# Layer 1's gated mixer: one output tile behind each block of products instead of two behind each pair

## The chip, the cores and the metric

The kernel is one program on one core of one Trainium2 chip. TensorE (PE) multiplies, with its weight loads shown apart as PEld; VectorE (DVE), ScalarE (ACT) and GpSimd (POOL) work on tiles in the on-chip memory SBUF and on the accumulators in PSUM; SyncE (SP) issues the DMA transfers from and to the device memory. Each engine takes its instructions in the order in which the program wrote them, and waits for other engines on semaphores. The metric is the device time of one execution in microseconds (us).

## The reference

The reference is one inference step of a two-layer trunk for 1024 prompt tokens and 8 x 8 = 64 sample tokens that share the weights, all in float32. Each layer has a token mixer and behind it a gated channel mixer (SwiGLU). The part that the change touches is the channel mixer of layer 1:

```
h = h + swiglu(rms_norm(h, norm_ffn_g[layer]), w_ffn_in[layer], w_ffn_out[layer])

def swiglu(h, w_in, w_out):
    g, u = jnp.split(h @ w_in, 2, axis=-1)
    return (jax.nn.silu(g) * u) @ w_out
```

The model width is 1024 and the hidden width 2816, which is 22 blocks of 128 hidden rows. Everything before it (attention with a paged cache, convolutions, pooling, layer 0's mixer) stays as it is.

## The kernel before

**Precision.** A float32 operand is kept as two parts that TensorE multiplies fast, a high part (a rounded copy, made by ACT) and a low part (the rest, a subtraction by POOL or DVE). A product takes three matmuls per 128 rows of the contraction: high weight times high data, high weight times low data, low weight times high data. So the low part of a weight is first read by the third matmul of a product.

**Groups.** The tokens run through layer 1's mixer in two groups, A (512 tokens, `GA`) and B (576 tokens, `GB`), one after the other, by `channel1`, which calls `run_ffn` (L456). Activations lie with channels on partitions and tokens along the free axis. The running sum `hb` stays in SBUF.

**A block of products.** For one block of 128 hidden rows, gate and up part together are a 2 x 2 block product, and `strassen` (L513) computes it with seven half-size products instead of eight. They go into four PSUM accumulators in this order: X (two products), Y (two), Z (two), W (one). Each product is 4 x 3 = 12 matmuls of 256 (A) or 288 (B) columns, so a block is 84. Seven adds on DVE (L525), an ACT copy (L537) and a Silu on ACT (L550) put the results together. `gated` leaves behind a POOL product of gate and up (L500) and a split of the result `hid` into high and low part (L240 on ACT, L241 on DVE); these are kept in the lists `post` and `late`, and `flush()` writes what is in them into the program.

**An output tile.** The hidden rows of two blocks are multiplied with a slice of `w_ffn_out` of 256 x 512: four quarter tiles of 128 output channels (`out_block`), each with its own accumulator, and behind each an add into `hb` (L295, `added`). The second slice covers the other 512 channels. Before the change, both output tiles of pair q-1 follow the two blocks of pair q. Three accumulators go round.

**Weights.** `loads` and `seq` hold the order in which weights are fetched and used; `add_ffn` writes that order for the channel mixer. SP fetches each slice into one of four `stage` buffers (L166). `w_split` turns them into `hl` tiles (three go round), which hold high and low parts. A block has four such entries r = 0 to 3, with seven half-tiles in all: for r = 0 DVE first makes three sums of gate and up weights (L200, L201, L202), then ACT and POOL cut them (L196, L197); r = 1 and 2 cut one more of the sums and three pieces of the fetched weights; r = 3 cuts one more sum (`sum_c`, L214). An output slice is cut in one piece by ACT and two by POOL (L184, L186). `w_next` hands out the next entry and splits ahead to two entries behind it:

```
    def w_next(live=0):
        j = wj[0]
        wj[0] += 1
        w_split(j + 3 - live)
        w_load(need(j + 6 - live))
```

While `thin[0]` is set, the three sums of an r = 0 entry aren't written at once but put into `parts_`, to be written one at a time.

**Side work.** `slot()` is called at fixed places, and every third call writes a piece of other work: in group A, pieces of group B's norm (L1683, DVE), in group B the squares of the finished tokens of A (L251 on ACT, L252 on POOL) and their final norm and output (L1881).

Of the kernel before, what the change touches and what calls it, by code (L numbers as in the profile page):

```python
# [22 lines left out]
NF = FFN // 128  # L23
# [34 lines left out]
def trunk_kernel(ctx, tc, x_prompt, x_sample, cache_k, cache_v, state_conformer, state_shortconv, state_pool,  # L58
# [19 lines left out]
    def tmp():  # L78
        return tmpbox[0].tile([128, tmpbox[1]], F, name="tmp")
# [15 lines left out]
    hb = hpool.tile([128, KC, T], F, name="hb")  # L95
# [9 lines left out]
    def add_load(src, kt):  # L105
        loads.append((src, kt))
        return len(loads) - 1

    def in_load(w, c0):
        return add_load(w.rearrange("(k p) n -> p k n", p=128)[:, :, c0:c0 + 128], 8)  # L110

    def add_in(w, c0):
        seq.append((in_load(w, c0), None, 0))

    def add_out(w, g, o):
        seq.append((add_load(w.rearrange("(k p) n -> p k n", p=128)[:, 2 * g:2 * g + 2, o * 512:o * 512 + 512], 2),
                    None, 0))

    def add_ffn(l, plain, both=True):
        for g in range(NF // 2):  # L120
            for f in (2 * g, 2 * g + 1):
                if f < plain:
                    add_in(w_ffn_in[l], f * 128)
                    add_in(w_ffn_in[l], FFN + f * 128)
                else:
                    a = in_load(w_ffn_in[l], f * 128), in_load(w_ffn_in[l], FFN + f * 128)
                    seq.extend(a + (r,) for r in range(4))
            if g and (g < NF // 2 - 1 or not both):
                for o in range(2):
                    add_out(w_ffn_out[l], g - 1, o)  # L130
        for o in range(2):
            if both:
                add_out(w_ffn_out[l], NF // 2 - 2, o)
            add_out(w_ffn_out[l], NF // 2 - 1, o)
# [38 lines left out]
    sums, parts_, thin = {}, [], [False]  # L173
# [46 lines left out]
    wj = [0]  # L220
# [6 lines that stand above are left out]
        return hls.pop(j)  # L227
# [65 lines left out]
    def added(g, dst, acc):  # L293
        for a, d in parts(g, acc, dst):
            dve.tensor_tensor(d, a, d, op=OP.add)  # L295
# [5 lines left out]
    def flush():  # L301
        todo = post + late
        post.clear()
        late.clear()
        for f in todo:
            f()
# [120 lines left out]
    def out_block(g, a, h, i, hh, first=True, last=True):  # L427
        for k in range(2):
            mm3(g, a, h[:, 0, k, i * 128:i * 128 + 128], h[:, 1, k, i * 128:i * 128 + 128], hh[:, k],
                first and k == 0, last and k == 1)  # L430
# [25 lines left out]
    def run_ffn(g, accs, ps, hidp, x, last, sig=False, slot=lambda: None, forms=None, plain=NF,  # L456
                free=lambda: None, hw=None, both=True):
        G = NF // 2
        n = g.n
        hid = {}  # L460
        gate = {}
        done = forms and "switch" not in forms

        def ev_g(a):
            t = tmp()
            if done:
                for p, o in parts(g, a, t):
                    act.activation(o, p, AF.Silu)
                gate["t"] = t
                return  # L470
            scaled(g, t[:, :n], a)
            if sig:
                s = tmp()
                act.activation(s[:, :n], t[:, :n], AF.Sigmoid)
                pool.tensor_tensor(t[:, :n], t[:, :n], s[:, :n], op=OP.mult)
            else:
                act.activation(t[:, :n], t[:, :n], AF.Silu)  # L477
            gate["t"] = t

        def to_hid(f):  # L480
            if f // 2 not in hid:
                hid[f // 2] = hidp.tile([128, 2, 2, hw or n], FR, name="hid")[:, :, :, :n]
            return hid[f // 2][:, f % 2]

        def ev_u(f, a):
            if done:
                t, dst = gate.pop("t"), to_hid(f)
                for p, o in parts(g, a, t):
                    dve.tensor_tensor(o, p, o, op=OP.mult)
                late.append(lambda: split(dst, t[:, :n]))  # L490
                return
            t = tmp()
            scaled(g, t[:, :n], a)
            gated(f, t, gate.pop("t"))

        def gated(f, t, u):
            dst = to_hid(f)

            def fin():
                (dve if both and f == NF - 1 else pool).tensor_tensor(t[:, :n], t[:, :n], u[:, :n], op=OP.mult)  # L500
                late.append(lambda: split(dst, t[:, :n], on=pool if sig else None))
            post.append(fin)

        def one(f, which):
            h = w_next()
            a = accs()
            block(g, a, h, x, K0[4:] + K0[:4] if done else K0, slot=slot)
            flush()
            ev_g(a) if which == 0 else ev_u(f, a)
            slot()  # L510

        def strassen(f):
            w2 = n // 2

            def prod(acc, h, i, b):
                for k in range(4):
                    xk = forms[b](k)
                    for s, (wi, xi) in enumerate(((0, 0), (0, 1), (1, 0))):  # L520
                        pe.matmul(acc[:, :w2], h[:, wi, i, k], xk[:, xi], start=k == 0 and s == 0,  # L521
                                  stop=k == 3 and s == 2)

            def add(out, acc, x):
                dve.tensor_tensor(out, acc[:, :w2], x, op=OP.add)  # L525

            a, b = slice(0, w2), slice(w2, n)
            X, h = accs(), w_next()
            prod(X[:, 0], h, 0, "t2")
            prod(X[:, 1], h, 1, "t3")  # L530
            flush()
            slot()
            Y, h = accs(), w_next()
            prod(Y[:, 0], h, 0, "t1")
            prod(Y[:, 1], h, 1, "b11")
            G_, U, P = tmp(), tmp(), tmp()
            act.activation(G_[:, a], Y[:, 1, :w2], AF.Copy)  # L537
            Z, h = accs(), w_next()
            prod(Z[:, 0], h, 0, "t4")
            add(U[:, a], X[:, 0], G_[:, a])  # L540
            add(U[:, b], X[:, 1], U[:, a])
            add(P[:, b], Y[:, 0], U[:, b])
            add(G_[:, b], Y[:, 0], U[:, a])
            prod(Z[:, 1], h, 1, "b21")
            W, h = accs(), w_next()
            prod(W[:, 0], h, 0, "b22")
            add(P[:, a], Z[:, 0], U[:, b])
            add(G_[:, a], Z[:, 1], G_[:, a])
            add(G_[:, b], W[:, 0], G_[:, b])
            act.activation(G_[:, :n], G_[:, :n], AF.Silu)  # L550
            gated(f, P, G_)
            slot()

        for q in range(G + 1):
            if q < G:
                for f in (2 * q, 2 * q + 1):
                    if f >= plain:
                        if f == plain:
                            forms.get("switch", forms.get("ready"))()
                        strassen(f)  # L560
                        continue
                    if f == 0 and not done:
                        run_in(g, accs, x, [ev_g, lambda a: ev_u(0, a)], norm_hooks(g, ps, at=(4, 7)), skew=3)
                        slot()
                        continue
                    one(f, 0)
                    one(f, 1)
            if q == G - 1:
                free()
                if both:  # L570
                    return last([hid.pop(q - 1), hid.pop(q)])
            if q == G:
                flush()
                flush()
                last(hid.pop(q - 1))
            elif q:
                hh = hid.pop(q - 1)
                for o in range(2):
                    thin[0] = True
                    h = w_next()  # L580
                    thin[0] = False
                    for i in range(4):
                        a = accs()
                        out_block(g, a, h, i, hh)
                        added(g, hb[:, o * 4 + i, g.cs], a)
                        if parts_:
                            parts_.pop(0)()
                        if o == 0 and i == 1:
                            flush()
                        slot()  # L590
# [45 lines left out]
    def accs():  # L636
        return accbox["p"].tile([128, len(accbox["g"].blocks), 512], F, name="acc")
# [1100 lines left out]
    for n in range(2, KC):  # L1738
        h = w_next()
        a = accs()  # L1740
# [4 lines left out]
    with tc.tile_pool(name="fab", bufs=1) as ep:  # L1745
        gen = forms_a(ep)
        for n in range(KC):
            h = w_next()
            a = accs()
# [256 lines left out]
```

## Time and profile before

| what | value |
|---|---|
| median of 3 runs | 2517.12 us (2516.61 to 2517.3) |
| profiled execution | 2522.03 us |
| its span, first to last instruction | 2519.8 us |
| mean granted TensorE clock | 0.992 |
| busy: PE / PEld / DVE / ACT / POOL | 96 / 87 / 66 / 44 / 64% of the span |
| moved by DMA | 258.32 MB, mean 103 GB/s |
| layer 1's channel mixer, group A, about | 1723 to 2103 us |
| the same, group B, about | 2103 to 2489 us |

In the rows that are shown below, L235 is the line of the helper that writes most matmuls (output tiles included), L521 that of the block products. A row of the timeline is start, duration, engine, line, operation, written tile <- read tiles, shapes, count, and in brackets the idle time of the engine just before it with what ended it. A row of the waits is: engine, tile and line that waited <- what it waited for: total us, times, longest. A row of the chain is start, duration, engine, tile and line. A row of the windows is the stretch, its length, then the busy time of PE, PEld, DVE, ACT and POOL (with counts), the granted clock, the DMA engines' busy share and GB/s.

### The profile page before, as it was taken

How to read it: one execution, taken by the hardware profiler on the slowest of the kernel's cores; microseconds unless marked ns; L12 is line 12 of the kernel's file. 1: busy time of each engine (PE TensorE's matmuls, PEld its weight loads, DVE VectorE, ACT ScalarE, POOL GpSimd, SP SyncE). 2: the span in 40 equal slices, each digit the busy share in tenths (PEclk: the TensorE clock that was granted, in tenths of full speed). 3: DMA queues.
4: the chain of work that ended last, by engine and by line, in shares of the span. 5: the costliest groups of instructions: out<-in, count | busy, mean ns of one | idle time of the engine just before them, and what ended most of it. 6: DMA issues, size and time to landing. Idle time of an engine off the chain costs nothing.

```text
span 2519.8 us, 41443 instructions
## 1 busy us (share of the span) xinstructions
PE 2427.2 (96%) x15871; PEld 2192.4 (87%) x15871; DVE 1664.8 (66%) x2301; ACT 1106.7 (44%) x1875; POOL 1619.5 (64%) x1263
## 2 busy tenths in 40 slices
PE   8999999999999999999999999998999999999998
PEld 6788877788777679999999899888888888999997
DVE  3696878977777653767565533458777679666655
ACT  5536776754444343343334422234333444443333
POOL 6664343655554576777778523267888886887775
PEclk9999999999999999999999999999999999999999
DMA  7332241234665534223232311252233333233322
GB/s 224 116 108 72 76 113 45 72 111 136 184 179 159 159 92 147 78 66 101 85 101 85 107 51 42 68 141 68 84 101 101 94 92 92 84 97 114 92 84 80
DMA packets 355486, 258.32 MB, mean 103 GB/s; under 512 B 22913, under 2 KB 303617, under 8 KB 355272
## 3 DMA queue, kind: packets, MB, share of 16 engines
q1 hardware_dynamic: 355256, 255.66, 34.5%
q8 instruction: 126, 2.06, 0.3%
q14 instruction: 72, 0.59, 0.1%
q10 hardware_dynamic: 32, 0.01, 0.0%
HBM read 237.41 MB, written 18.69 MB: 102 GB/s over the span
## 4 chain that ended last, share of the span: by engine, by line
PE 43%; DVE 10%; POOL 3%; issue 2%; ACT 1%; POOLq 0%; DVEq 0%; ACTq 0%
PE acc L235 22%; PE acc L521 19%; DVE sum L200 2%; POOL hl L197 2%; DVE hb L295 1%; DVE hid L241 1%; DVE sum L201 1%; DVE sum L202 1%; DVE b L1686 0%; DVE tmp L525 0%; POOL tmp L500 0%; DVE sum_c L214 0%; DVE fb L1690 0%; PE blk L1909 0%; DVE x L1686 0%
## 5 line engine op out<-in xcount | busy, mean ns | idle before, releaser
L186 POOL TENSOR_TENSOR hl<-stage,hl 128x512 fp32r<-128x512 f32 x464 | 633.7, 1390 | 395.7 <-ACT hl L184 287.4
L235 PE MATMUL acc<-x,hl 128*128 128x512 f32 (+1 forms) x3648 | 774.3, 350 | 12.9 <-DVE tmp L291 3.0
L235 PEld LDWEIGHTS acc<-x,hl 128*128 128x128 f32 x3648 | 588.3, 190 | 77.7 <-issue 6.2
L235 PE MATMUL acc<-hid,hl 128*128 128x288 f32 (+1 forms) x3096 | 550.3, 333 | 13.0 <-DVE hb L295 5.5
L235 PEld LDWEIGHTS acc<-hid,hl 128*128 128x128 f32 x3096 | 471.5, 190 | 66.7 <-DVE hb L295 7.9
L295 DVE TENSOR_TENSOR hb<-acc,hb 128x512 f32<-128x512 f32 (+1 forms) x360 | 256.2, 718 | 175.2 <-PE acc L235 174.1
L521 PE MATMUL acc<-x,hl 128*128 128x288 f32 (+1 forms) x2676 | 362.2, 290 | 3.4 <-POOL hl L197 2.3
L521 PEld LDWEIGHTS acc<-x,hl 128*128 128x128 f32 x2676 | 349.0, 188 | 5.7 <-POOL hl L197 3.1
L197 POOL TENSOR_TENSOR hl<-sum,hl 128x512 fp32r<-128x512 f32 x180 | 237.2, 1346 | 176.3 <-ACT hl L196 176.3
L184 ACT ACTIVATE hl<-stage 128x1024 fp32r<-128x1024 f32 x232 | 243.4, 1054 | 229.3 <-PE acc L235 140.5
L525 DVE TENSOR_TENSOR tmp<-acc,tmp 128x288 f32<-128x288 f32 (+1 forms) x420 | 173.6, 442 | 230.3 <-ACT tmp L537 135.3
L197 POOL TENSOR_TENSOR hl<-stage,hl 128x512 fp32r<-128x512 f32 x180 | 268.5, 1514 | 13.0 <-ACT hl L196 12.9
L521 PE MATMUL acc<-b,hl 128*128 128x256 f32 (+1 forms) x1548 | 216.5, 291 | 14.9 <-DVE tmp L525 12.0
L521 PEld LDWEIGHTS acc<-b,hl 128*128 128x128 f32 x1548 | 202.2, 189 | 20.5 <-ACT hl L196 12.9
L235 PE MATMUL acc<-x1t,hl 128*128 128x288 f32 x1152 | 216.3, 296 | 1.5 <-POOL hl L186 1.5
L235 PEld LDWEIGHTS acc<-x1t,hl 128*128 128x128 f32 x1152 | 195.9, 188 | 19.5 <-POOL hl L186 1.7
L196 ACT ACTIVATE hl<-sum 128x512 fp32r<-128x512 f32 x180 | 103.1, 623 | 242.2 <-DVE sum L202 219.4
L291 DVE TENSOR_TENSOR tmp<-acc,rr 128x512 f32<-128x512 f32 (+1 forms) x108 | 75.2, 710 | 139.7 <-PE acc L235 122.6
L196 ACT ACTIVATE hl<-stage 128x512 fp32r<-128x512 f32 x180 | 105.5, 618 | 67.8 <-PE acc L235 62.7
L500 POOL TENSOR_TENSOR tmp<-tmp 128x576 f32<-128x576 f32 (+1 forms) x85 | 125.6, 1477 | 9.3 <-ACT tmp L477 8.3
L252 POOL TENSOR_TENSOR ss<-ss,tmp 128x512 f32<-128x512 f32 (+1 forms) x69 | 107.0, 1551 | 29.0 <-ACT tmp L251 18.8
L235 PE MATMUL acc<-x1a,hl 128*128 128x512 f32 x480 | 122.4, 409 | 2.9 <-POOL hl L186 1.3
(293 smaller groups left out, 3177.4 us busy)
## 6 DMA issues: line engine op xcount, KB each, us to landing
stage<-in_w_ffn_in_dram SPq DMA_DIRECT2D x176, 512.0 KB
stage<-in_w_ffn_out_dram SPq DMA_DIRECT2D x88, 512.0 KB
stage<-in_w_in_even_dram SPq DMA_DIRECT2D x40, 512.0 KB
kst<-in_cache_k_dram SPq DMA_DIRECT2D x64, 256.0 KB
vst<-in_cache_v_dram SPq DMA_DIRECT2D x56, 256.0 KB
stage<-in_w_out_even_dram SPq DMA_DIRECT2D x16, 512.0 KB
stage<-in_w_in_odd_dram SPq DMA_DIRECT2D x16, 512.0 KB
stage<-in_w_out_odd_dram SPq DMA_DIRECT2D x16, 512.0 KB
```

Source lines behind the costliest of these rows:

```text
L184: act.activation(hl[:, 0], st, AF.Copy)
L186: pool.tensor_tensor(hl[:, 1, c], st[:, c], f32(hl[:, 0, c]), op=OP.subtract)
L196: act.activation(hl[:, 0, c], x, AF.Copy)
L197: pool.tensor_tensor(hl[:, 1, c], x, f32(hl[:, 0, c]), op=OP.subtract)
L200: todo = [lambda: dve.tensor_tensor(sb, su[:, lo], su[:, hi], op=OP.add), lambda: dve.tensor_tensor(sa[:, hi], sg[:, lo], su[:, lo], op=OP ...
L235: pe.matmul(acc[:, b, :c1 - c0], w, xs[:, xi, c0 - o:c1 - o], start=first and s == 0, stop=last and s == 2)
L252: pool.tensor_tensor(ss[:, g.cs], ss[:, g.cs], t[:, :g.n], op=OP.add)
L291: dve.tensor_tensor(d, a, r, op=OP.mult)
L295: dve.tensor_tensor(d, a, d, op=OP.add)
L500: (dve if both and f == NF - 1 else pool).tensor_tensor(t[:, :n], t[:, :n], u[:, :n], op=OP.mult)
L521: pe.matmul(acc[:, :w2], h[:, wi, i, k], xk[:, xi], start=k == 0 and s == 0, stop=k == 3 and s == 2)
L525: dve.tensor_tensor(out, acc[:, :w2], x, op=OP.add)
```

## The change

Layer 1 now works on one output tile behind each block: behind block 2q the first slice of pair q-1, behind block 2q+1 the second. In the diff `alt` marks the pairs for which this holds: layer 1, q = 1 to 9 in group A (whose last two pairs' outputs are done together, as before) and q = 1 to 10 in group B, 18 and 20 blocks. Layer 0 keeps its order (`done` is set in layer 1 only). `add_ffn` writes the weights in the new order. The three sums for the next block are put into `parts_` when W's weights are handed out; the first is written at the end of the block, the second and third behind the first two quarter tiles' adds. In the output tile `w_next(1)` splits one entry less ahead, and the next one is split at the third quarter. A second `flush()` stands ahead of W in all blocks of layer 1.

```
     def add_ffn(l, plain, both=True):
         for g in range(NF // 2):
+            outs = g and (g < NF // 2 - 1 or not both)
             for f in (2 * g, 2 * g + 1):
...
                     seq.extend(a + (r,) for r in range(4))
-            if g and (g < NF // 2 - 1 or not both):
+                if outs and l:
+                    add_out(w_ffn_out[l], g - 1, f % 2)
+            if outs and not l:
                 for o in range(2):
                     add_out(w_ffn_out[l], g - 1, o)
...
-        def strassen(f):
+        def part():
+            if parts_:
+                parts_.pop(0)()
+
+        def out_tile(hh, o):
+            h = w_next(1)
+            for i in range(4):
+                a = accs()
+                out_block(g, a, h, i, hh)
+                added(g, hb[:, o * 4 + i, g.cs], a)
+                if i == 0:
+                    flush()
+                if i < 2:
+                    part()
+                if i == 2:
+                    w_split(wj[0] + 2)
+                slot()
+
+        def strassen(f, outs=False):
...
             prod(Z[:, 1], h, 1, "b21")
+            if done:
+                flush()
+            thin[0] = outs
             W, h = accs(), w_next()
+            thin[0] = False
...
             gated(f, P, G_)
+            if outs:
+                part()
             slot()
 
         for q in range(G + 1):
+            alt = done and 0 < q < G - both
...
-                        strassen(f)
+                        strassen(f, alt)
+                        if alt:
+                            out_tile(hid[q - 1], f % 2)
...
+            elif alt:
+                hid.pop(q - 1)
             elif q:
```

No engine gets more or fewer matmuls, sums, cuts, adds or loads; lines of the changed kernel are numbered 3 higher in the weight code (L200 becomes L203) and 21 to 25 higher in the block code (L525 becomes L546).

DVE, a steady pair of group A, from the last output adds of one pair to the first of the next, before the change (L295 adds a quarter tile into `hb`, L525 are a block's seven adds):

```order
L202 TENSOR_TENSOR sum_19662<-sum_19663,stage 128x512
L295 TENSOR_TENSOR hb<-acc,hb 128x512 x5
L214 TENSOR_TENSOR sum_c<-stage,sum_19662 128x512
L241 TENSOR_TENSOR hid<-tmp,hid 128x512
L200 TENSOR_TENSOR sum_19816<-stage 128x512
L201 TENSOR_TENSOR sum_19815<-stage 128x512
L202 TENSOR_TENSOR sum_19815<-sum_19816,stage 128x512
L525 TENSOR_TENSOR tmp<-acc,tmp 128x256 x7
```

and in the changed kernel, from a block's adds to the next block's:

```order
L546 TENSOR_TENSOR tmp<-acc,tmp 128x256 x7
L203 TENSOR_TENSOR sum_19681<-stage 128x512
L298 TENSOR_TENSOR hb<-acc,hb 128x512
L204 TENSOR_TENSOR sum_19680<-stage 128x512
L298 TENSOR_TENSOR hb<-acc,hb 128x512
L205 TENSOR_TENSOR sum_19680<-sum_19681,stage 128x512
L298 TENSOR_TENSOR hb<-acc,hb 128x512 x2
L217 TENSOR_TENSOR sum_c<-stage,sum_19680 128x512
L244 TENSOR_TENSOR hid<-tmp,hid 128x512
L546 TENSOR_TENSOR tmp<-acc,tmp 128x256 x7
```

The three sums no longer stand ahead of a block's adds; they stand between the adds of the output tile, and two quarter tiles' adds follow the third sum, where five did.

POOL, the same place, before the change, a whole pair (L197 cuts a block's weights, L186 the output slices, L500 is the product of gate and up):

```order
L197 TENSOR_TENSOR hl<-sum_20003,hl 128x512 x2
L197 TENSOR_TENSOR hl<-sum_20004,hl 128x512
L197 TENSOR_TENSOR hl<-stage,hl 128x512 x3
L197 TENSOR_TENSOR hl<-sum_c,hl 128x512
L197 TENSOR_TENSOR hl<-sum_20156,hl 128x512 x2
L197 TENSOR_TENSOR hl<-sum_20157,hl 128x512
L197 TENSOR_TENSOR hl<-stage,hl 128x512 x3
L500 TENSOR_TENSOR tmp<-tmp 128x512
L197 TENSOR_TENSOR hl<-sum_c,hl 128x512
L186 TENSOR_TENSOR hl<-stage,hl 128x512 x4
L500 TENSOR_TENSOR tmp<-tmp 128x512
```

and in the changed kernel, a half:

```order
L200 TENSOR_TENSOR hl<-sum_19850,hl 128x512 x2
L200 TENSOR_TENSOR hl<-sum_19851,hl 128x512
L200 TENSOR_TENSOR hl<-stage,hl 128x512 x3
L200 TENSOR_TENSOR hl<-sum_c,hl 128x512
L189 TENSOR_TENSOR hl<-stage,hl 128x512 x2
L503 TENSOR_TENSOR tmp<-tmp 128x512
```

Each block's seven cuts are now followed by the two cuts of one output slice and by the product of its own block, ahead of the next block's cuts.

## The prediction

> **What bounds the kernel now.** I read the page first: TensorE is busy 96% of the span and leads the chain of waits.
>
> ```profile
> PE 2427.2 (96%) x15871; PEld 2192.4 (87%) x15871; DVE 1664.8 (66%) x2301; ACT 1106.7 (44%) x1875; POOL 1619.5 (64%) x1263
> PE 43%; DVE 10%; POOL 3%; issue 2%; ACT 1%; POOLq 0%; DVEq 0%; ACTq 0%
> ```
>
> Only layer 1's mixer changes, so next the windows of its two token groups, A (512 tokens) and B (576), in steady pairs.
>
> ```profile
> 1861.00:2060.00 199.00, 193.28 (x1304) 173.43 (x1303) 140.78 (x194) 77.62 (x132) 163.74 (x121) 1.00 0.33 96
> 2129.00:2240.00 111.00, 109.54 (x814) 108.03 (x814) 76.84 (x106) 46.22 (x78) 99.01 (x71) 1.00 0.30 90
> 2240.00:2489.00 249.00, 248.45 (x1872) 248.22 (x1870) 156.19 (x228) 94.90 (x154) 191.63 (x141) 1.00 0.32 97
> ```
>
> The columns are PE, PEld, DVE, ACT and POOL busy, clock, DMA. PE stands idle 5.7 us of 199 in A, 1.5 of 111 early in B, 0.5 of 249 later: B is bound by TensorE, so there the change has nothing to win. The rows of the chain give the lengths:
>
> ```profile
> 1892.85 1.78 DVE hid L241
> 1944.71 11.50 PE acc L235 x48
> 2057.88 1.78 DVE hid L241
> ...
> 2347.97 22.32 PE acc L521 x168
> 2370.30 12.80 PE acc L235 x96
> ```
>
> From the first to the last DVE row lie five pairs of A: 33.0 us a pair, 16.5 a half (one block and one output tile). B's half is (22.32+12.80)/2 = 17.56; one output matmul of B takes 0.133, one quarter tile 1.6. What A waits for is in the waits of PE from 1725 to 2090:
>
> ```profile
> PE acc L521 <- DVE tmp L525: 11.2, 12, 2.9
> PE acc L521 <- POOL hl L197: 4.1, 6, 1.7
> PE acc L235 <- DVE hb L295: 2.8, 6, 0.8
> ```
>
> The largest has its place in the timeline, before the seventh product W of a pair's first block:
>
> ```profile
> 1894.53 1.58 PE L521 MATMUL acc<-b,hl 128*128 128x256 f32 x12
> 1894.55 1.78 DVE L200 TENSOR_TENSOR sum<-stage 128x512 f32<-128x512 f32 x1
> 1895.95 1.57 PE L521 MATMUL acc<-x,hl 128*128 128x256 f32 x12
> 1898.55 2.39 DVE L525 TENSOR_TENSOR tmp<-acc,tmp 128x256 f32<-128x256 f32 x6
> 1899.57 1.66 PE L521 MATMUL acc<-b,hl 128*128 128x256 f32 x12 [0.61 <-DVE tmp L525]
> ```
>
> W needs the accumulator that the adds of L525 empty, and these queue on DVE behind the three weight sums of the next block. A product of 12 matmuls starts every 1.42 us, so a block of seven is 9.9, an output tile 11.5/2 = 5.75, and an A half without waits 15.65. The whole stall is 16.5-15.65 = 0.85 a half, over 18 halves 15 us: the most that can be won.
>
> **The change part by part.** Counts of matmuls, sums, cuts and loads stay. *Removed:* the three sums ahead of L525. *Moved:* they now stand, for every block, one behind L525, one behind each of the first two quarter tiles' adds into hb. Before, one restart in two had eight quarter tiles behind it, and the other ran during the block; now every restart has four. So I follow that chain in the rows of B's output stage:
>
> ```profile
> 2405.25 12.96 PE L235 MATMUL acc<-hid,hl 128*128 128x288 f32 x96
> 2407.05 0.76 DVE L295 TENSOR_TENSOR hb<-acc,hb 128x576 f32<-128x576 f32 x1 [1.14 <-PE acc L235]
> 2407.55 1.42 POOL L500 TENSOR_TENSOR tmp<-tmp 128x576 f32<-128x576 f32 x1
> 2409.44 0.74 DVE L295 TENSOR_TENSOR hb<-acc,hb 128x576 f32<-128x576 f32 x1
> 2410.11 0.67 DVE L201 TENSOR_TENSOR sum<-stage 128x512 f32<-128x512 f32 x1
> 2412.04 0.68 DVE L202 TENSOR_TENSOR sum<-sum,stage 128x512 f32<-128x512 f32 x1
> 2413.54 3.80 POOL L197 TENSOR_TENSOR hl<-sum,hl 128x512 fp32r<-128x512 f32 x3 [4.58 <-ACT hl L196]
> 2418.05 2.16 PE L521 MATMUL acc<-x,hl 128*128 128x288 f32 x15
> ```
>
> A quarter tile's add starts 0.2 behind its last matmul (2405.25+1.6 to 2407.05) and frees DVE after 0.67; the first low cut starts 1.5 behind the start of the third sum (2412.04 to 2413.54), a cut takes 1.27. Now the cut is 4.5 ahead of the next block. After the change, counted from the first output matmul: second quarter ends 3.2, its add 3.4 to 4.07, third sum 4.07, low cut 5.57 to 6.84. The next block starts at 6.4 and its third matmul, the first to read a low part, is due at 6.67: it **waits 0.2**. The second sum may be held by the product L500, so I take 0.25, over B's 20 halves **+5 us** (bounds 0 and 0.9 each, the latter below).
>
> In A the quarters are shorter (5.75/4 = 1.44) while DVE and POOL are not:
>
> ```profile
> 1911.48 0.42 DVE L525 TENSOR_TENSOR tmp<-acc,tmp 128x256 f32<-128x256 f32 x1 [0.98 <-PE acc L521]
> 1911.94 0.63 ACT L550 ACTIVATE tmp<-tmp 128x512 f32<-128x512 f32 x1 [1.09 <-DVE tmp L525]
> 1913.64 3.11 DVE L200 TENSOR_TENSOR sum<-stage 128x512 f32<-128x512 f32 x1
> 1914.92 1.28 POOL L500 TENSOR_TENSOR tmp<-tmp 128x512 f32<-128x512 f32 x1
> ```
>
> Output starts at 1911.28 there (1911.48 less the 0.2), so the last add and the Silu end 1.3 after it, and the product L500 runs 1.35 to 2.65. The first hb add is over at 2.3, the second sum held until 2.65 and done at 3.25, the second hb add until 3.9, the third sum at 3.9, the low cut 5.4 to 6.7. Due: 5.75+0.24 = 6.0. A **wait of 0.7**. Behind it POOL gives a cut every 1.27 and PE uses one every 1.42, but two DVE instructions (sum_c and the split of hid) hold POOL on the way:
>
> ```profile
> 1891.07 4.72 POOL L197 TENSOR_TENSOR hl<-stage,hl 128x512 fp32r<-128x512 f32 x3
> 1891.07 1.86 DVE L214 TENSOR_TENSOR sum_c<-stage,sum 128x512 f32<-128x512 f32 x1
> 1892.85 1.78 DVE L241 TENSOR_TENSOR hid<-tmp,hid 128x512 fp32r<-128x512 f32 x1
> ```
>
> Three cuts took 4.72 instead of 3.80, 0.46 per holder. The fourth cut then ends at 5.4+5.07+0.92 = 11.4; with X late by 0.7 it is due at 5.75+0.7+3x1.42+0.24 = 10.95: a second wait of 0.45. An A half becomes 15.65+0.7+0.45 = 16.8; hand-overs of 0.05 each bring me to 16.9, against 16.5 now: **+0.4 x 18 = +7 us**. Bounds: only the first wait, 0.6, makes 16.25 (-4 us in all); a second sum or first sum that loses to L500 twice, as the 3.11 us of L200 above, adds 0.9 (+23).
>
> The Trainium skill (SBUF — State Buffer, Who interferes with whom) says that a DVE instruction with two SBUF inputs and a GpSimd instruction reading SBUF exclude each other and that the first to issue has the port for one whole instruction. By that rule the sum at 1913.64 would have waited for one cut only, about 1.8 us, and the upper bound would be nothing; the row shows a wait for two. By the row the upper bound stays.
>
> *Side work, moved too.* In A's first halves DVE makes eight pieces of B's norm, two in a half; in B's first halves seven squares are added on POOL, two in a half:
>
> ```profile
> 1787.17 1.45 DVE L1683 SCALAR_TENSOR_TENSOR xs<-hb,par,rr 128x576 f32<-128x576 f32 x1
> 2217.32 1.27 POOL L252 TENSOR_TENSOR ss<-ss,tmp 128x512 f32<-128x512 f32 x1
> ```
>
> The first of a half now stands behind the first sum, or ahead of L500, and delays the restart by up to 1.45 or 1.27; the second stands among the cuts. Both already cost something now (B's 1.5 idle). A: **+1** (0 to 7). B: four halves by 1.27 to 2.5, less 1.5: **+5** (0 to 9).
>
> *At nothing:* the extra flush ahead of W finds its lists empty except in the first and last blocks of a group, where one split of hid (1.78 at most) goes ahead of three adds that the next block needs only at its third product. *Loads:* three now share four stage buffers, so the up half for the next block is fetched once a buffer is free behind the fifth cut:
>
> ```profile
> 1904.89 2.53 POOL L197 TENSOR_TENSOR hl<-stage,hl 128x512 fp32r<-128x512 f32 x2
> 1906.20 1.62 SPq L166 DMA_DIRECT2D stage<-in_w_ffn_in_dram  x2
> 1906.00:1907.00 1.00, 1.00 (x11) 1.00 (x10) 0.00 (x0) 0.10 (x1) 1.00 (x2) 1.00 0.00 0
> 1907.00:1912.00 5.00, 4.95 (x39) 4.62 (x39) 2.79 (x7) 2.35 (x4) 5.00 (x5) 1.00 0.73 212
> ```
>
> Issue at 1906.20, nothing before 1907, then two loads (1.06 MB) in under 5 us: one lands about 3.5 behind its issue (estimate from these rows). In A the fifth cut ends at 5.4+6.35+0.92 = 12.7, the load lands at 16.2, the first sum comes at 16.9+0.6 = 17.5. Cover 1.3 us; gone, each us costs one a half.
>
> Sum: 7+5+1+5 = **+18 us**. The profiled execution (2522.03, span 2519.8) would be 2540; it lies 4.9 above the median shown, so the median 2517.12 becomes **2535**.
>
> **Rivals.** *Faster, 16%:* the restart's first low cut decides. If it lands before the third matmul in both groups (in A 0.7 earlier than worked out, say because the hb adds and sums close up), only the gain is left: 15.75 a half in A, -0.75 x 18 = -13.5, time 2504. For it: DVE is busy 140.78 of 199 us only, and the stall removed is real. Against: each link is a measured row, and they run in order on one engine. *No change, 15%:* A's two waits cost what W's did, B hides its 0.2: 2519. For it: 0.4 and 0.25 a half are small against the rows' scatter. *Much slower, 10%:* the first sum loses to the product or the load comes late in every half: 0.9 x 38 = 34 on top of the forecast, 2569. For it: the 3.11 row. Against: now POOL pauses there. That the change doesn't do what it says is out: the order shows one tile behind each block.
>
> **How the numbers follow.** Forecast 59%: 2535, its own range 2523 to 2549. About 5 us (0.2%) can be told from no change here. Slower 59+10 = 69%, same 15%, faster 16%. The range runs from 2510 (A at its lower bound and B at nothing give 2513; a little further, it takes in part of the fast rival) to 2553 (A at +23, the rest about as forecast), and leaves out the rest of the fast rival and the worst: under two in ten.
>
> **What would show it.** Right: waits of PE on L525 gone; in their place PE's block line waiting for POOL's cuts, in both groups, at X and at the second product of Y; A's pair 33.5 to 34, B's 35.5 to 36; PE idle in B's steady windows 1 to 2% where it was 0.2%. Wrong: B's pair still 35.1, or A's below 32.5; or a third sum that starts less than 3.5 us behind the output tile's first matmul.

## The result and the profile after

| what | before | after |
|---|---|---|
| median | 2516.8 us (2513.98 to 2517.3, 6 runs) | 2530.91 us (2530.29 to 2534.55, 6 runs) |
| ratio | | 1.006, 95% interval 1.0049 to 1.0071 |
| profiled execution, its span | 2522.03, 2519.8 | 2531.25, 2529.4 |
| granted TensorE clock | 0.992 | 0.993 |
| group A of layer 1's mixer | 379.25 | 383.05 |
| group B | 381.95 | 390.40 |

The change makes the kernel 14 us slower. A is counted here from the first product on `b` (before: row of 1728.19 us) to the end of the last norm rows that hand group B over (`DVE hid ... x4`), B from there to the first `PE blk` row. For the changed kernel the first of these is, in the timeline,

```profile
1725.65 1.58 PE L542 MATMUL acc<-b,hl 128*128 128x256 f32 x12
```

and the other two, in the chain of waits (start, duration, engine, tile, line),

```profile
2105.97 2.73 DVE hid L1718 x4
...
2499.10 2.51 PE blk L1941 x18
```

A lost 3.8 us and B 8.45. Both sum to 12.3, while the two spans differ by 9.6: code that the change doesn't touch, ahead of layer 1's mixer, ran 2.5 us shorter in the profiled execution after (first row at 1725.65, before at 1728.19). So the loss in the mixer, not the difference of spans, goes with the 14 us of the medians (12 to 18 by the interval).

The busy times on the page of the changed kernel:

```profile
PE 2433.7 (96%) x15871; PEld 2196.4 (87%) x15871; DVE 1616.9 (64%) x2301; ACT 1101.7 (44%) x1875; POOL 1616.3 (64%) x1263
```

DVE is busy 48 us less (1616.9 for 1664.8) with the same 2301 instructions: the three weight sums of all blocks take 175.0 us instead of 236.4 (L203 to L205 for L200 to L202), since they meet POOL's instructions for a shorter time, as I read it. The program is slower all the same, as DVE's busy time was not what set the end. The windows, the same three stretches as before:

```profile
1861.00:2060.00 199.00, 191.81 (x1274) 173.39 (x1273) 118.56 (x192) 75.74 (x131) 159.14 (x119) 1.00 0.32 96
2129.00:2240.00 111.00, 106.39 (x779) 103.52 (x778) 67.15 (x102) 45.46 (x76) 91.19 (x68) 1.00 0.27 82
2240.00:2489.00 249.00, 247.94 (x1850) 245.59 (x1850) 155.09 (x228) 90.69 (x153) 189.17 (x139) 1.00 0.33 97
```

PE is idle 7.2 us of 199 in A (5.7 before), 4.6 of 111 early in B (1.5) and 1.1 of 249 later (0.55). What it waits for is in the waits of PE, from 1725 to 2095 us (A):

```profile
PE acc L542 <- POOL hl L200: 15.1, 20, 1.6
PE acc L542 <- DVE tmp L546: 2.9, 1, 2.9
```

and from 2095 to 2500 us (B):

```profile
PE acc L542 <- POOL hl L200: 3.9, 7, 0.8
```

W's wait for the adds on DVE has gone from 11.2 us to 2.9 (one time only); the wait for POOL's cuts has grown from 4.1 to 15.1 in A and from 0.3 to 3.9 in B. One half of A, in the timeline, from the output tile's first matmul on:

```profile
1932.41 5.78 PE L238 MATMUL acc<-hid,hl 128*128 128x512 f32 x24
1932.95 0.68 DVE L203 TENSOR_TENSOR sum<-stage 128x512 f32<-128x512 f32 x1
1933.78 1.30 POOL L503 TENSOR_TENSOR tmp<-tmp 128x512 f32<-128x512 f32 x1 [0.75 <-ACT tmp L575]
1934.62 1.01 DVE L204 TENSOR_TENSOR sum<-stage 128x512 f32<-128x512 f32 x1
...
1936.15 0.68 DVE L205 TENSOR_TENSOR sum<-sum,stage 128x512 f32<-128x512 f32 x1
1937.65 4.25 POOL L200 TENSOR_TENSOR hl<-sum,hl 128x512 fp32r<-128x512 f32 x3 [2.57 <-ACT hl L199]
1938.02 0.40 PE L542 MATMUL acc<-x,hl 128*128 128x256 f32 x2
1938.99 1.50 PEld L542 LDWEIGHTS acc<-x,hl 128*128 128x128 f32 x12 [0.77 <-POOL hl L200]
1940.72 2.67 PEld L542 LDWEIGHTS acc<-x,hl 128*128 128x128 f32 x22 [0.24 <-POOL hl L200]
```

The third sum (L205) starts 3.74 us behind the output tile, the low cut 1.50 behind that. X's first two matmuls need no low part and run at 1938.02; the third is held until 1938.99, and POOL stood idle for 2.57 us just before its cut. A second, smaller wait of the weight loads comes at X's second product. The chain gives the length of a half in A, from one stalled X to the next, and then in B:

```profile
1922.16 1.70 PE acc L542 x12
...
1938.99 1.71 PE acc L542 x12
...
2245.89 11.16 PE acc L542 x84
...
2319.12 11.19 PE acc L542 x82
...
2337.08 11.19 PE acc L542 x82
```

16.83 us in A. In B 17.96 where the block starts with a wait (82 matmuls behind it, two ahead), and no wait where the output tile carries transposes of other work (the block runs 84 in one piece at 2245.89). B's longest halves are those with squares on POOL, whose blocks stall twice (chain):

```profile
2167.53 5.91 PE acc L542 x42
2173.43 1.25 POOL hl L200
2174.72 4.78 PE acc L542 x34
...
2187.22 5.90 PE acc L542 x42
```

2167.53 to 2187.22 is 19.7 us.

### The profile page after: what moved, and what is told of

It is laid out like the page before. It is cut to its first block, busy times and chain, and to the rows that moved or that the text cites. A ratio compares the mean times of both kernels' runs of the same rounds, so it can differ in the third digit from the quotient of the medians.

```text
span 2529.4 us, 41386 instructions
## 1 busy us (share of the span) xinstructions
PE 2433.7 (96%) x15871; PEld 2196.4 (87%) x15871; DVE 1616.9 (64%) x2301; ACT 1101.7 (44%) x1875; POOL 1616.3 (64%) x1263
## 4 chain that ended last, share of the span: by engine, by line
PE 44%; DVE 8%; POOL 3%; ACT 2%; issue 1%; ACTq 0%; POOLq 0%; DVEq 0%
PE acc L542 24%; PE acc L238 19%; POOL hl L200 2%; DVE hb L298 2%; DVE sum L204 1%; ACT hl L199 1%; DVE sum L205 1%; DVE b L1718 0%; DVE fb L1722 0%; POOL hl L189 0%; PE blk L1941 0%; DVE x L1718 0%; DVE xs L1722 0%; DVE fa L1715 0%; DVE sum L203 0%
## 5 line engine op out<-in xcount | busy, mean ns | idle before, releaser
L189 POOL TENSOR_TENSOR hl<-stage,hl 128x512 fp32r<-128x512 f32 x464 | 635.5, 1392 | 387.5 <-ACT hl L187 280.2
L542 PE MATMUL acc<-x,hl 128*128 128x288 f32 (+1 forms) x2676 | 379.2, 293 | 21.9 <-POOL hl L200 18.5
L298 DVE TENSOR_TENSOR hb<-acc,hb 128x512 f32<-128x512 f32 (+1 forms) x360 | 257.7, 719 | 165.0 <-PE acc L238 164.1
L200 POOL TENSOR_TENSOR hl<-sum,hl 128x512 fp32r<-128x512 f32 x180 | 249.9, 1415 | 159.7 <-ACT hl L199 159.7
L546 DVE TENSOR_TENSOR tmp<-acc,tmp 128x288 f32<-128x288 f32 (+1 forms) x420 | 175.3, 442 | 275.2 <-ACT tmp L558 180.0
L200 POOL TENSOR_TENSOR hl<-stage,hl 128x512 fp32r<-128x512 f32 x180 | 260.1, 1469 | 8.9 <-ACT hl L199 8.9
L503 POOL TENSOR_TENSOR tmp<-tmp 128x576 f32<-128x576 f32 (+1 forms) x85 | 124.5, 1465 | 46.0 <-ACT tmp L575 36.7
L244 DVE TENSOR_TENSOR hid<-tmp,hid 128x576 fp32r<-128x576 f32 (+1 forms) x66 | 92.2, 1397 | 36.5 <-ACT hid L243 35.8
```

The source lines that it names most:

```text
L189: pool.tensor_tensor(hl[:, 1, c], st[:, c], f32(hl[:, 0, c]), op=OP.subtract)
L200: pool.tensor_tensor(hl[:, 1, c], x, f32(hl[:, 0, c]), op=OP.subtract)
L244: (on or dve).tensor_tensor(dst[:, 1], src, f32(dst[:, 0]), op=OP.subtract)
```

## The experiments

**The theory**: the new order costs what the late restart of the low cuts costs, in both groups. **Rivals**: the loss lies in the new place of the output tiles themselves (loads, accumulators); it comes from the side work; the second flush matters. All runs in one table; A and B are counted as above, from each run's own profile. Where an expectation below names lengths of A and B, these were counted to the start of the `DVE hid` row, which makes A shorter and B longer by the length of that row, 2.7 us in some runs and 3.7 in others (the change's own 2.73, A alone 3.67).

| kernel | median us | ratio to before, 95% interval | A | B |
|---|---|---|---|---|
| before | 2515.4 to 2518.6 | 1 | 379.25 | 381.95 |
| the change | 2530.91 | 1.0060 (1.0049 to 1.0071) | 383.05 | 390.40 |
| new order in A only | 2522.56 | 1.0021 (1.0011 to 1.0031) | 383.4 | 382.9 |
| new order in B only | 2518.46 | 1.0007 (0.9997 to 1.0017) | 371.0 | 390.4 |
| sums ahead of the output tile | 2512.83 | 0.9983 (0.9974 to 0.9993) | 368.7 | 387.1 |
| sums one quarter later | 2593.33 | 1.0307 (1.0290 to 1.0324) | 413.5 | 421.2 |
| the second flush alone | 2510.17 | 0.9968 (0.9952 to 0.9983) | 370.4 | 382.8 |
| sums ahead, new order in A only | 2508.49 | 0.9961 (0.9947 to 0.9975) | 368.7 | 382.0 |
| the change, squares added on DVE | 2529.53 | 1.0044 (1.0027 to 1.0061) | 382.9 | 389.1 |
| the change, low weights last | 2521.86 | 1.0016 (1.0006 to 1.0027) | 380.3 | 384.3 |
| sums ahead and low weights last | 2512.98 | 0.9987 (0.9978 to 0.9996) | 368.6 | 387.9 |
| the same, new order in A only | 2507.98 | 0.9970 (0.9959 to 0.9980) | 368.2 | 381.7 |
| second flush and low weights last | 2509.06 | 0.9974 (0.9965 to 0.9983) | 369.1 | 382.2 |

The first four experiments ran with the same runs of before (median 2516.3 us), the next four with others (2518.57), the last three with others again (2515.42), so ratios are compared across them, not medians.

### Sums ahead, and sums later

The place of the three sums is the disputed cause, so it was moved both ways, with nothing else changed. Ahead:

```
             gated(f, P, G_)
-            if outs:
+            while outs and parts_:
                 part()
```

> The changed kernel, but all three weight sums stand directly behind the block's seven adds, ahead of the first quarter's add. Theory: the third sum then starts about 2.65 us behind the first output matmul in A (held by the product of gate and up) and 2.85 in B, instead of 3.75 and 4.1; the first low cut starts at 4.2 and 4.35 instead of 5.24 and 5.6, before it is due. X waits no more: an A half goes from 16.83 to 15.7 to 15.9 (-17 to -20 us over 18), a B half from 17.95 to 17.57 (-7.6 over 20), time 2500 to 2506, faster than both kernels. Rival (the sums wait for the load of the up weights, three loads sharing four buffers): the sums can't start earlier, nothing changes, 2531. Rival (the hb adds, pushed back by 1.3 us, hold an accumulator): X or the third quarter waits for L298 instead, 2515 to 2531.

Measured 2512.83 us, ratio 0.9983: 18 us less than the change, and faster than before, but 7 us above the upper end of what was expected. A fell by 14.3 us, B by 3.3; a steady half in A became 16.08 us, not the 15.7 to 15.9 expected. In B's steady halves the wait is gone (chain: output tile and block follow each other without a piece of POOL between):

```profile
2286.81 11.16 PE acc L542 x84
2297.97 6.40 PE acc L238 x48
```

17.56 us a half, TensorE's time without a wait. What stays in B are the halves with squares: weight loads there, 2120 to 2240 us, still wait for cuts (and once, 2.4 us, for the squares themselves):

```profile
PEld acc L542 <- POOL hl L200: 3.9, 6, 0.9
```

Later: no sum at the end of the block, one behind each of the first three quarter tiles.

```
-                if i < 2:
+                if i < 3:
                     part()
...
             gated(f, P, G_)
-            if outs:
-                part()
```

> The changed kernel, but each of the three weight sums one quarter later: behind the first, second and third quarter's adds. Theory: the chain moves by one quarter, 1.44 us in A and 1.6 in B, and as X already waits, all of it is paid: 18 x 1.44 + 20 x 1.6 = 58 us, less what the halves with squares hide, 2580 to 2590. Load rival: the third sum isn't what X waits for, at most 10 us more, below 2541.

Measured 2593.33 us, 62 more than the change, a little above what was expected. Its timeline, A:

```profile
1947.14 5.77 PE L238 MATMUL acc<-hid,hl 128*128 128x512 f32 x24
...
1952.15 0.68 DVE L205 TENSOR_TENSOR sum<-sum,stage 128x512 f32<-128x512 f32 x1
...
1953.63 0.50 PE L542 MATMUL acc<-x,hl 128*128 128x256 f32 x2 [0.72 <-ACT hl L199]
1953.66 4.19 POOL L200 TENSOR_TENSOR hl<-sum,hl 128x512 fp32r<-128x512 f32 x3 [3.85 <-ACT hl L199]
1955.42 5.61 PEld L542 LDWEIGHTS acc<-x,hl 128*128 128x128 f32 x34 [1.49 <-POOL hl L200]
```

The third sum starts 5.01 behind the output tile where it was 3.74, the cut 6.52 where it was 5.24, and the loads for the third matmul wait 1.49 where it was 0.77. Beside that the high part now comes late too: X's first matmul waits 0.72 for ACT. The chain gives the halves:

```profile
1937.35 9.96 PE acc L542 x82
1955.42 11.52 PE acc L542 x82
```

A half in A is 18.07 us (1937.35 to 1955.42) where it was 16.83, a stalled half in B 19.63 (2463.46 to 2483.09) where it was 17.95: 1.24 and 1.68 more, near the quarter tile's 1.44 and 1.6 that the theory adds.

Not all of the 62 us is this, though. In eight halves of A the 82 matmuls behind the wait took some 11.5 us, as in the second row, where the same work took 9.96 in the others: 12 us in all. In such a stretch, 1957 to 1959 us, the granted clock was 0.50; from 1939 to 1941 it was 1.00. Over 1725 to 2105 us it was 0.96, in the change 0.99; in B it was 1.00 in both. So of A's 30 us some 18 are waits and 12 are the lower clock, and of the 61 us of both groups 49 go with the place of the sums. That the total lies so near the expected 58 is in part luck. Why the clock fell in these halves and not in the others is not shown.

The place of the sums sets the waits in both directions, for A and for B. The rival that the new place of the output tiles itself costs is out for A, which with the sums ahead is shorter than before, and no longer than the old order with the second flush (below); in B 5 us stay, in the halves with squares.

### One group at a time

```
-            alt = done and 0 < q < G - both
+            alt = done and 0 < q < G - both and both
```

and `not both` for B, with the weights' order to match. The second flush stays in both groups.

> The new order in group A alone; group B keeps two output tiles behind each pair (the second flush stays in both). Theory (each block's restart waits for the first low cut, which hangs on the third sum): in the two profiles, counted from the first block product of layer 1 (1723.45 before, 1720.88 after), group A is 3.8 us longer and group B 8.5. So 4 us over before, about 2521. Rival (the cost is the same in each of the 38 halves, whatever its quarters' length): 14.1 x 18/38 = 6.7, about 2523.5. If the gain and the loss in A were both large and cancelled otherwise than worked out, it could lie below before.

> The new order in group B alone; group A keeps the old one. Theory: 8.5 us over before, about 2525, of which some 5 are the four halves with squares on POOL (19.7 us long instead of 17.6) and the rest 0.38 in the steady halves. Even-cost rival: 14.1 x 20/38 = 7.4, about 2524. With the run of group A alone the two should add up to about 14 us.

A alone gave 2522.56 us, 6.3 above its runs of before (2.8 to 7.8 by the interval), which holds the theory's 4 and the even-cost rival's 6.7 alike; the traces go with the theory, A 4.2 us longer and B 0.9. B alone gave 2518.46, 6.5 below what was expected, and the two add up to 8.4 us over before where the whole change gave 14. The profile shows why: B was as long as in the change (390.4), but A, in its *old* order, was 8.2 us shorter than before. The only thing new there is the second flush, which the prediction had priced at nothing.

### The second flush

```
             prod(Z[:, 1], h, 1, "b21")
+            if done:
+                flush()
             W, h = accs(), w_next()
```

in the kernel before, and nothing else.

> The kernel before with one edit of the change alone: the second flush ahead of W in layer 1's blocks; the order of tiles and sums stays. In the profile of the run with the new order in B alone, group A (old order with this flush) took 368.3 us where before took 376.5 (first product of layer 1 to the low parts of B's operands), a pair 31.75 instead of 33.0; in the run with the new order in A alone, group B (old order with this flush) took 386.6 instead of 384.7. Theory (the flush does it: the split of hid moves from among the output tile's adds to ahead of W): 8.2 less, 1.9 more, about 2510. Rival (those shorter lengths came with the other group's order, by the loads ahead): 2516, no change.

Measured 2510.17 us, ratio 0.9968, as expected. Its waits of PE, 1722 to 2090 us:

```profile
PE acc L521 <- DVE tmp L525: 5.1, 6, 2.9
```

and three rows of its timeline:

```profile
1885.13 1.35 DVE L214 TENSOR_TENSOR sum_c<-stage,sum 128x512 f32<-128x512 f32 x1
...
1893.13 1.66 PE L521 MATMUL acc<-b,hl 128*128 128x256 f32 x12 [0.16 <-DVE tmp L525]
...
1902.95 1.11 DVE L241 TENSOR_TENSOR hid<-tmp,hid 128x512 fp32r<-128x512 f32 x1
```

The split of `hid` (of the pair's first block, 1902.95) now runs among the last adds of the second block instead of among the output adds. W's waits fell from 11.2 us to 5.1, and at the place that the prediction showed from 0.61 to 0.16: sum_c ahead of the three sums took 1.35 us there, 1.86 before. The traces show where this comes from. Counted from the pair's first output matmul, the third sum starts at 6.88 us (1879.37 against 1872.49) where it started at 7.79 (1885.81 against 1878.02), so POOL's next three cuts from `stage` start 0.32 us behind X (1884.65 against 1884.33) instead of 0.81 (1891.07 against 1890.26), and sum_c waits only for the rest of the first of them. Two things make the third sum earlier: the split (0.68) no longer stands ahead of it, and the first sum, L200, meets less of POOL's work: in the six steady pairs it took 3.11 us four times and 1.85 to 1.87 twice, and now takes about 1.85 three times and 0.68 three times. Why it meets less is not shown. So most of what the new order could win, W's wait, was to be had in the old order for one line. Seen from this kernel the new order costs 383.05-370.4 = 12.7 us in A and 390.4-382.8 = 7.6 in B, 20 in all. The changed kernel without the flush was not tried: behind a group's first changed block the output tile reads a `hid` that only this flush splits in time.

### The new order where it can win

```
-            alt = done and 0 < q < G - both
+            alt = done and 0 < q < G - both and both
...
-            if done:
+            if done and both:
                 flush()
...
-            if outs:
+            while outs and parts_:
                 part()
```

New order, flush and sums ahead in A alone; B exactly as before.

> The best of the pieces so far: in group A the new order with all three sums directly behind the block's adds, and the second flush; group B exactly as before. In the profiles group A took 366.0 us with the sums ahead, 376.5 before. Theory (the groups add up): 10.5 below before, 2506, faster than both kernels and than the run with the sums ahead in both groups (2513), in which B took 389.9 against 384.7. Rival (the groups don't add up, as the runs of A and B alone didn't: 6.2 + 2.2 against 14.1): 2510 to 2514.

Measured 2508.49 us, ratio 0.9961: faster than both kernels, 22 us less than the change, and 10.1 below its own runs of before, as the theory had it (10.5). A is 368.7, against 370.4 with the flush alone; the intervals of the two times overlap, so that by the times the new order is worth nothing that can be told beside the flush, and by the traces 1.7 us.

### Squares

```
-        pool.tensor_tensor(ss[:, g.cs], ...)
+        (on or pool).tensor_tensor(ss[:, g.cs], ...)
```

with `on=dve` for the squares of group A that run in B.

> The changed kernel, with the seven adds of squares in B's first halves on DVE instead of POOL. Theory (on POOL the first of a half holds the product of gate and up, and with it the second and third sum, and the second stands among the cuts): four halves of 19.7 us shrink by 1 to 1.5 each, as the DVE add is short, 4 to 6 us below the changed kernel, 2525 to 2527. Rival (these halves are long for the Squares on ACT or the sums' port): 2531, no change. If DVE's own queue is the bound, up to 3 us slower.

Measured ratio 1.0044; its interval overlaps that of the change, so the time decides nothing. The trace says more: B is 1.3 us shorter, under the 4 to 6 that were expected. Its chain, one half:

```profile
2161.83 1.50 DVE ss L255
...
2168.02 11.21 PE acc L542 x82
...
2187.16 11.23 PE acc L542 x82
```

The second stall within the block is gone, but on DVE the square (1.50) stands ahead of the first output add and delays the same restart: 19.14 us a half instead of 19.7, against 17.96 without squares. A square cost on both engines tried, since the restart chain passes through both.

### Low weights last

A rival way to take the wait away, without moving a sum: each block product does its eight matmuls with high weights first, then the four with low ones, so that the low cut is due at the ninth matmul instead of the third (in layer 1 only).

```
-                for k in range(4):
-                    xk = forms[b](k)
-                    for s, (wi, xi) in enumerate(((0, 0), (0, 1), (1, 0))):
+                steps = [(k, s) for k in range(4) for s in ((0, 0), (0, 1), (1, 0))]
+                if done:
+                    steps.sort(key=lambda t: t[1][0])
...
```

> The changed kernel, but in layer 1's block products the four matmuls with the low weight parts come last of the twelve, instead of every third (same matmuls, another order of summing). Theory (X and Y wait for the low cut): it is due at the ninth matmul instead of the third, 0.7 us later in A and 0.8 in B, which is about what X waits (0.72 and 0.34): the A half falls from 16.83 to 15.7 to 16.1, the B half from 17.95 to 17.57, together 13 to 28 us below the changed kernel, 2503 to 2518. Rival (X waits for the high cut on ACT, the accumulators or the loads): 2531, no change.

Measured 2521.86 us, ratio 1.0016: 9 us less than the change (11 by the ratios), where 13 to 28 were expected. In B it did what was expected: 17.56 us a half, 6.1 us in all. In A a steady half fell only from 16.83 to 16.48, the four beside group B's norm grew from 17.75 to 18.1, and A as a whole fell by 2.8. The loads' waits, 1850 to 2070 us:

```profile
PEld acc L238 <- POOL hl L189: 6.2, 12, 0.5
```

The wait has moved from X to the output tile's own low cut (L189), two cuts behind the block's seven. So in A the waits were not only a matter of which cut is due first: the cuts as a whole are late.

### Both together

Three kernels put the low weights last on top of the sums ahead (both groups, and A only) and of the flush alone.

> The changed kernel with both mends: the three weight sums are written at the end of the block, ahead of the output tile, and each block product reads its four low weights last. If the forecast's mechanism (the restart of the low cuts) is all that the new order costs, both groups lose what is left of it: A about 4 us shorter than with the sums ahead alone (366.0, of which 6.6 us were waits for low cuts), B's squares halves lose their waits (389.9 to about 386): 2504 to 2507 us. Rival: POOL's own loop of nine cuts and a product is the bound, so that the waits only move to the output tile's low cut; then nothing is gained on 2513.

> New order with the sums ahead in group A alone, group B in the old order, low weights last in all block products of layer 1. B should stay at 384.7 us, since nothing waits for low cuts there in the old order. A as in the run with both mends, about 362 instead of 366: 2504 to 2505 us. Rival (POOL's loop bounds A): 2508.5, as without the low weights last.

> The old order with the flush ahead of W and the low weights last. The old order waited 4.1 us in A for POOL's cuts; with the low weights last most of it should go: 2506 to 2508 us, against 2510 with the flush alone. If it equals the run with the new order in A, the new order itself is worth nothing beside the flush.

Measured 2512.98, 2507.98 and 2509.06 us, ratios 0.9987, 0.9970 and 0.9974: each the same, within its interval, as without the low weights last. The rival written down for the first two (POOL's loop is the bound) was right, and my theory's 4 us did not come. The third equals the new order in A alone within the intervals, which by its own condition says that the new order is worth nothing beside the flush. The first of the three has this window in A:

```profile
1861.00:2060.00 199.00, 197.44 (x1353) 179.09 (x1352) 133.85 (x196) 83.25 (x140) 169.62 (x125) 1.00 0.32 97
```

these waits of POOL, 1850 to 2070 us:

```profile
POOL hl L200 <- ACT hl L199: 30.9, 12, 2.6
```

and this chain:

```profile
1928.45 5.84 PE acc L543 x48
...
1944.51 5.84 PE acc L543 x48
```

POOL is busy 169.6 us of 199 and waits about 30 for the restart's high cut on ACT, 2.6 in each half; nothing else is left of its time. A half (1928.45 to 1944.51) is 16.06 us, of which 2.6 are that restart and 13.5 are nine cuts, the product and its collisions with DVE. With the sums ahead and the matmuls in their old order it is 16.08. So with the sums ahead A is bound by POOL's loop, its work and its one restart, and the order of TensorE's matmuls no longer matters.

## Why the prediction was right, and where not

2535 was forecast (2510 to 2553) and 2530.9 measured, with the sign and the mechanism named: the third sum behind the second quarter tile's add makes the low cut late for the third matmul of the next block. The range of 43 us would have held a change without any loss too, so the hit in time says little by itself; the rows of the chain say more. The forecast's terms add up to 18 us, 8 in A and 10 in B; the traces have 3.8 and 8.45. A's term was twice too large, and that the total is still near is owed to B's.

- **The restart chain.** Forecast from the rows of before: third sum 4.07 us behind the output tile in B, low cut 5.57 to 5.65; in A low cut 5.4. Measured in A 3.74 and 5.24 (rows above), and in B:

```profile
2401.93 6.56 PE L238 MATMUL acc<-hid,hl 128*128 128x288 f32 x48
...
2404.41 0.96 DVE L204 TENSOR_TENSOR sum<-stage 128x512 f32<-128x512 f32 x1
...
2406.01 0.68 DVE L205 TENSOR_TENSOR sum<-sum,stage 128x512 f32<-128x512 f32 x1
2407.52 4.25 POOL L200 TENSOR_TENSOR hl<-sum,hl 128x512 fp32r<-128x512 f32 x3 [2.70 <-ACT hl L199]
2408.87 4.56 PEld L542 LDWEIGHTS acc<-x,hl 128*128 128x128 f32 x34 [0.34 <-POOL hl L200]
```

  4.08 and 5.59. The chain was right to 0.2 us in both groups, with the second sum held by the product L503 (0.96 and 1.01 us instead of 0.68) as forecast.
- **A, a half.** Forecast 16.9 from 16.5, measured 16.83 in the twelve steady halves. The first wait was forecast at 0.7 and is 0.77. The second was forecast at 0.45 at Y's second product; it is 0.24, at X's second.
- **A, side work: wrong.** The forecast took the steady halves' +0.4 for all 18 and added 1 us for the pieces of group B's norm. The first row of X of the 18 changed blocks and that of the X behind the last, before and then in the change:

```profile
1752.65 4.75 PE L521 MATMUL acc<-x,hl 128*128 128x256 f32 x36
...
2055.30 4.43 PE L521 MATMUL acc<-x,hl 128*128 128x256 f32 x36
...
1749.69 5.15 PE L542 MATMUL acc<-x,hl 128*128 128x256 f32 x36
...
2055.86 0.40 PE L542 MATMUL acc<-x,hl 128*128 128x256 f32 x2
```

  That is 302.65 us before, 16.81 a half and not 16.5, and 306.17 after: A lost 3.5 there, not 8. The twelve steady halves went from 16.53 to 16.83 (X at 1856.99 and 1853.88 is where they begin), all of the loss; the six beside group B's norm from 17.39 to 17.37. So the step that failed is "+0.4 x 18" plus 1. In those six halves W's waits were larger before: of the 11.2 us, 4.3 fall after 1850 us, 2.9 are one wait that stays, and 4.0 are left for them. The new order took these away too, and paid for it with a longer wait at X (1.2 us in four of the six).
- **B, steady.** Forecast 0.25 x 20 = 5. Measured 0.38 in 11 halves that stall (0.4 longer than 17.56), 4.2 in all; four halves with transposes in the output tile give the sums time and don't stall, which the forecast overlooked (18.43 us each, of which 0.88 is the transposes').
- **B, squares.** Forecast +5 for four halves. The four from the X at 2166.17 to that at 2245.73 took 79.56 us; before they took 75.00 (2164.77 to 2239.77), 4.6 less. The second stall within the block is as forecast ("the second stands among the cuts").
- **Loads.** Forecast to be covered by 1.3 us. In the half shown the first sum starts at 1932.95 without a wait named before it, so the cover held there.
- **The flush "at nothing".** In the changed kernel nothing shows against it, but the old order had 8 us to gain by it. The sum of the forecast stands, since it was counted from the old kernel as it was; the reading that a win on W's wait has to come from moving the sums does not. The bound of 15 us for the gain was counted from steady halves too; by 16.81 a half it is 21. The best kernel here is 8 to 10 us faster.
- **Rivals.** Faster, at 2504, needed the low cut to come before the third matmul in both groups. With the sums ahead this holds in B's steady halves, and the time was 2512.8: A then met POOL's loop, which no rival named.

Right signs that were named: A's pair 33.5 to 34 (33.66), B's 35.5 to 36 (35.9), W's waits gone. Not met: PE idle 1 to 2% in B's steady window; it is 0.4%. Ten of that window's 14 halves stall for 0.38 us, 1.5% of it; but the row of X's 36 matmuls with a wait inside takes 5.33 us instead of 4.96 and counts as busy.

## What to carry to other kernels

Where a chain of engines restarts once per block, count it from the event that releases it to its first use, in rows, for the shortest stretch that will stand between them: an order that puts other engines' work into that stretch cost its length once per steady half here, and the chain was right to 0.2 us. Take the length before from all blocks that the change touches, not from the steady ones alone: that was the term that failed. When a change comes with a small companion edit, run that alone first: here it was worth 8 us, and the change a loss. And when a wait is taken away by reordering its consumer, look for the loop behind it: if the producer is busy for all of the period but its restart, the wait moves instead of going.

## What the runs showed of the hardware

- A sum of two SBUF operands on DVE took 0.68 us alone, and 0.96 to 1.01 when issued 0.8 to 1 us into a POOL product of 1.30 to 1.42: it waited for the rest of that one instruction (1934.62 against 1933.78+1.30 = 1935.08 in A). The Trainium skill (SBUF — State Buffer, Who interferes with whom) says the same, an exclusion for one whole instruction; these rows agree, where the 3.11 us row of before had not. Adds of the same size with one operand in PSUM (L298, 0.68 to 0.69 in all 77 of layer 1's A) show no such stretch.
- With the sums a quarter later, TensorE waits up to 2 us in each half of A (0.72 and 1.28); in eight of the halves the 82 matmuls behind that took 11.5 us instead of 9.96, and the granted clock was lower among them (0.50 from 1957 to 1959 us). In the change, with waits of 0.8 and 0.2, it was 1.00 from 1861 to 2060 us.
- The same unchanged code, about 1700 us up to the first product on `b`, ended between 1722.95 and 1728.19 us in the nine profiled executions that have the matmuls in their old order. For differences of that size the stage has to be compared, not the span.
